# A hybrid decoder layer on one core: quarter sums of x made among the attention pairs, splits ordered behind bank copies, mixer weights split in the memory gates, mixer begun by halves

## The chip, the cores and the metric

The kernel runs on one core of one Trainium2 chip, and the metric is the device time of one execution in microseconds, where less is better. A core has TensorE (PE, the matrix products; its weight loads are listed as PEld), VectorE (DVE), ScalarE (ACT), GpSimd (POOL) and SyncE (SP), which each work through a list of their own in order. SP and POOL also issue the DMA transfers of this kernel. Products land in PSUM, in eight banks of 128 x 512 float32 numbers.

## The reference

The layer takes x (512 tokens of 1024) and a memory of 256 rows, all in float32:

```python
u = rms_norm(h, ln_mix_pre[l])
proj = jnp.einsum('bsd,de->bse', u, w_in[l])
qa, ka, va, qb, kb, vb, qm, gl = jnp.split(proj, split_idx, axis=-1)
y_swa = swa_sink_attention(...)        # banded, 8 heads in 2 key groups, sinks, relative bias
y_sb = stick_breaking_attention(...)   # 8 heads
y_mem = memory_cross_attention(...)    # 4 heads over 256 memory rows
g = jax.nn.sigmoid(gl.reshape(B, S, N_BRANCH, D))
merged = (g[:, :, 0] * jnp.einsum('bse,ed->bsd', y_swa, w_branch_swa[l])
          + g[:, :, 1] * jnp.einsum('bse,ed->bsd', y_sb, w_branch_sb[l])
          + g[:, :, 2] * jnp.einsum('bse,ed->bsd', y_mem, w_branch_mem[l]))
mix = jnp.einsum('bsd,de->bse', merged, w_out[l])
h = h + rms_norm(mix, ln_mix_post[l])
u = rms_norm(h, ln_ffn_pre[l])
a = jax.nn.silu(jnp.einsum('bsd,df->bsf', u, w_gate[l])) * jnp.einsum('bsd,df->bsf', u, w_up[l])
ffn = jnp.einsum('bsf,fd->bsd', a, w_down[l])
h = h + rms_norm(ffn, ln_ffn_post[l])
```

## The kernel before, in words

**Products in three.** TensorE multiplies in a float32 form of reduced width (`F32R`). Every operand is therefore split into a high part (a cast on ScalarE) and a low part (raw minus high, on VectorE), by `split` (L134), and a product is made as three (`mm3`, L166 to L170): high by high, high by low, low by high. `after(ins, first)` (L180) adds an ordering edge: `ins` comes later than `first` where both stand on one engine's list.

**The stream.** A `Stream` (L33) holds units in a list. A unit has a weight to load, its split, and a generator that issues its products and says how many microseconds of TensorE each piece is worth. `ahead` runs loads four units ahead and splits three ahead (two for the last branch weights); `begin` functions of a unit run just before its products. `run(us)` issues so many microseconds of products, and `until(flag)` runs to a marked unit. The attention heads are generators as well: they issue their scores and softmax, then give a number of microseconds for the stream's products to fill, then go on with transposes and outputs. The program is written in this order, and a planner then makes each engine's list from it by its own estimates, with the earlier written work first where both are ready.

**Order of the stages.** Projections for the stick-breaking heads come first, then those heads (`sb_head`, L824) among the remaining projections, the memory keys and values and the stick-breaking branch's gates. Then four pairs of banded heads (`swa_pair`, `yield 10.0` and `yield 2.0`) run among `qm` (four units), the stick-breaking branch (`branch_sb`, four units) and the first gate units. Then come the two memory pairs (`mem_pair`) among the banded branch's gates and products, then the memory branch's gates and products, the mixer, and the feed-forward network.

**Gates by quarters.** The banded and the memory branch's gates (1024 x 1024 weights) are multiplied by a scheme of seven products of quarters in place of eight: p1, p2, p5, p3, p6, p7, p4 (`QUART`), each with two units (c = 0, 1) of 12 products (`quart`), 2.7 us. Left sides are quarters of u or sums of quarters of the scaled x (`q_sum1` to `q_sum4`: scalings on ScalarE, L467, and accumulating DMAs issued by POOL); `q_parts` splits those sums. Right sides are quarters of the weight; the later ones are made by accumulating DMAs over the raw tile of an earlier one (`q_issue`, L449), which must wait until that one has been split. p1, p6, p7 and p4 go on in the banks called x, p5 and p3 in y, p2 in w; where a bank is gone on with, its state is first copied out by ScalarE (`q_end`, L534). In the banded branch the quarter sums serve both branches' gates: x quarters are loaded when the weights of units 2 and 3 of the gates are loaded, and sums and splits hang on the units -1 to 7, counted from the first gate unit (`g0`).

**Branches, merge, mixer.** `branch_t` multiplies the banded and memory outputs by the branch weights for each half h of the columns and each of four token tiles t, multiplies by the gate on VectorE (L583), and for the memory branch adds the banded branch's part on POOL or, for the last tile, on VectorE (L586). `merge(h)` transposes the sum on TensorE (L597), adds the stick-breaking part on VectorE (L601) and splits the result into `merged` (tiles `mgh`, `mgl`). `mix(t)` multiplies a token tile by the two halves of `w_out` (eight `mm3` each), and goes on with norm and residual. The mixer's weights are loaded into the stream's staging buffers (`wp`, four of each kind) and split by `out_load` and `out_split` after the flag `gates_late`.

**Memory.** Nearly all tiles of 128 x 512 come from one pool of 71 (`ckp`). PSUM has two pools, of two banks (`dps`) and six (`aps`).

Of the kernel before, what the change touches and what calls it, by code (L numbers as in the profile page):

```python
# [105 lines left out]
def tile_kernel(ctx, tc, a):  # L106
# [3 lines left out]
    ckp = ctx.enter_context(tc.tile_pool(name="ckp", bufs=71))  # L110
# [55 lines left out]
    def mm3(out, l, r, start, stop):  # L166
        (lh, ll), (rh, rl) = l, r
        nc.tensor.matmul(out, lh, rh, start=start, stop=False, skip_group_check=True)  # L168
        nc.tensor.matmul(out, lh, rl, start=False, stop=False, skip_group_check=True)  # L169
        nc.tensor.matmul(out, ll, rh, start=False, stop=stop, skip_group_check=True)  # L170
# [330 lines left out]
    def q_parts(p):  # L501
        for c in range(2):
            t = quarter.pop((p, c))
            if p == "p7":

                for k in range(2):
                    h, l = cols(u[2 * c + k], 256, 256)
                    split(t[:, k * 256 : (k + 1) * 256], h, l)
            else:
                qsum[(p, c)] = parts(f"xs{p}{c}", t)  # L510
# [19 lines left out]
    def q_end(b, p, i):  # L530
        ps = qbank[(QBANK[p], i)]
        if p in ("p1", "p5", "p6", "p7"):
            t = qkeep[(p, i)] = ck(f"gq{b}{p}{i}")
            nc.scalar.copy(t[:, :], ps[:, :])  # L534
# [16 lines left out]
    def quart(b, p, c):  # L551
        def gen(hi, lo):
            for i in range(2):
# [4 lines left out]
                for k in range(2):  # L558
                    mm3(qbank[key][:, :], q_left(p, c, k, i), cols((hi, lo), k * 512, 512), first and k == 0, c == 1 and k == 1)
# [6 lines left out]
    def branch_t(b, h, q):  # L566


        def gen(hi, lo):
# [3 lines left out]
            for t in range(NT):  # L573
# [10 lines left out]
                if b == MEM:  # L584
                    eng = nc.vector if t == NT - 1 else nc.gpsimd
                    eng.tensor_tensor(g[:, :], g[:, :], gate_t[(SWA, t, h)][:, :], op=ALU.add)  # L586
                    if (h, t) == (1, 0):
# [4 lines left out]
    def merge(h):  # L592

        for c in range(4):
            pt = aps(f"mg{h}{c}")
# [1034 lines left out]
```

## Time and profile before

| | |
|---|---|
| Median of three runs | 807.53 us (807.14 to 809.06) |
| The profiled execution | 808.21 us |
| Its span, first to last instruction | 806.4 us |
| Mean granted TensorE clock in it | 0.999 |
| TensorE busy | 792.4 us, 98% |
| VectorE, ScalarE, GpSimd busy | 608.1, 474.5, 106.4 us |
| DMA | 123.43 MB, 149 GB/s over the span |

The profile is of one execution, with the time of every instruction on every engine. A row of the groups has the line of the kernel that issued it, the engine, the operation, the tiles written and read (numbers of buffers left out), the shape and the count; then the busy time and the mean, and the idle time of the engine ahead of it with what ended it. Rows in order of time begin with start and duration in us. The ends of matrix products are modelled, so that the busy time of TensorE overstates how full it is; the distances between starts tell more. The 128 x 512 products that follow each other undisturbed start 0.23 us apart. The granted clock was full in all slices of the page.

### The profile page before, as it was taken

To read this page: it belongs to the slowest core of one execution; us is meant where nothing else is said; L and a number is where in the kernel's file an instruction comes from. 1 tells how busy PE (TensorE), PEld (TensorE's weight loads), DVE (VectorE), ACT (ScalarE), POOL (GpSimd) and SP (SyncE) were. 2 spreads that over 40 slices of the span, in tenths; PEclk is the share of its full clock that TensorE was granted. 3 is DMA by queue.
4 is the path that set the end of the run, shared out by engine and by line. 5 is a ranking of instruction groups with operands and counts; after the bars stand their busy time and mean duration, and the time that the engine had idled before them with its cause. 6 is when DMAs were issued, how large, how long until landed. Compare 5 with 4: busy or idle time off the path is not lost.

```text
span 806.4 us, 12444 instructions
## 1 busy us (share of the span) xinstructions
PE 792.4 (98%) x4694; PEld 695.6 (86%) x4694; DVE 608.1 (75%) x957; ACT 474.5 (59%) x847; POOL 106.4 (13%) x131
## 2 busy tenths in 40 slices
PE   9999999999999989999999999999999999999996
PEld 6899888778788868888778899999999999988885
DVE  6994877556588866775787579877676767898797
ACT  7562776556655686565844466654444444666673
POOL 1203200000000240002044200110000000205200
PEclk9999999999999999999999999999999999999999
DMA  8444535121123798339789806987767662859802
GB/s 296 141 128 134 185 105 157 54 78 53 53 79 105 158 193 204 91 70 176 255 275 304 156 1 174 265 203 203 190 179 192 171 170 74 192 124 228 202 0 104
DMA packets 41724, 123.43 MB, mean 153 GB/s; under 512 B 4928, under 2 KB 6640, under 8 KB 41664
## 3 DMA queue, kind: packets, MB, share of 16 engines
q1 hardware_dynamic: 29760, 86.32, 33.3%
q0 software_dynamic: 11472, 35.93, 24.1%
q8 instruction: 36, 0.59, 0.3%
q10 hardware_dynamic: 432, 0.39, 0.1%
q14 instruction: 24, 0.20, 0.1%
HBM read 116.85 MB, written 3.67 MB: 149 GB/s over the span
## 4 chain that ended last, share of the span: by engine, by line
PE 90%; DMA 3%; DVE 3%; issue 2%; ACT 1%; POOL 0%; DVEq 0%; POOLq 0%; ACTq 0%
PE gx L168 5%; PE gx L170 5%; PE gx L169 5%; PE z L173 4%; PE gy L170 3%; PE gy L168 3%; PE gy L169 3%; PE x L170 2%; PE x L169 2%; PE x L168 2%; PE br L169 2%; PE br L168 2%; PE br L170 2%; PE mx L170 2%; PE mx L169 2%
## 5 line engine op out<-in xcount | busy, mean ns | idle before, releaser
L136 ACT CAST hi<-gw 128x1024 fp32r<-128x1024 f32 x77 | 79.9, 1048 | 83.0 <-DVE gw L1212 39.6
L137 DVE TENSOR_TENSOR lo<-raw,hi 128x1024 fp32r<-128x1024 f32 (+2 forms) x76 | 91.9, 1210 | 41.1 <-ACT hi L136 41.1
L137 DVE TENSOR_TENSOR lo<-gw,hi 128x1024 fp32r<-128x1024 f32 x77 | 93.5, 1223 | 33.2 <-ACT hi L136 33.0
L136 ACT CAST hi<-raw 128x1024 fp32r<-128x1024 f32 (+2 forms) x76 | 78.4, 1037 | 55.5 <-PE pv L170 10.5
L1194 POOL DMA_DIRECT2D gw<-in_w_gu x27 | 23.3, 939 | 195.7 <-DMA gw<-in_w_gu 60.7
L136 ACT CAST hi<-r 128x1024 fp32r<-128x1024 f32 (+1 forms) x24 | 23.6, 982 | 19.8 <-PE y L170 5.3
L169 PE MATMUL x<-lo,lh 128*128 128x512 f32 x88 | 34.3, 389 | 0.0
L168 PE MATMUL x<-hi,lh 128*128 128x512 f32 x88 | 34.2, 389 | 0.0
L170 PE MATMUL x<-hi,ll 128*128 128x512 f32 x88 | 34.1, 390 | 0.0
L137 DVE TENSOR_TENSOR lo<-r,hi 128x1024 fp32r<-128x1024 f32 (+1 forms) x24 | 27.1, 1131 | 3.6 <-ACT hi L136 3.5
L186 ACT ACTIVATE e<-e 128x384 f32<-128x384 f32 (+1 forms) x48 | 26.9, 561 | 1.5
L137 DVE TENSOR_TENSOR lo<-bp,hi 128x512 fp32r<-128x512 f32 x33 | 22.6, 720 | 5.9 <-ACT hi L136 5.8
L136 ACT CAST hi<-bp 128x512 fp32r<-128x512 f32 x33 | 19.3, 620 | 13.1 <-PE y L170 4.8
L449 POOL DMA_DIRECT2D raw<-in_w_g x16 | 14.6, 976 | 90.8 <-DVE lo L137 74.1
L858 DVE SCALAR_TENSOR_TENSOR e<-z,e 128x384 f32<-128x384 f32 (+1 forms) x24 | 14.3, 598 | 15.7 <-ACT e L186 15.7
L170 PE MATMUL mx<-woh,mgl 128*128 128x512 f32 x64 | 25.1, 392 | 0.4 <-DVE mgl L137 0.4
L168 PE MATMUL g<-uh,hi 128*128 128x512 f32 x64 | 25.4, 398 | 0.0
L170 PE MATMUL g<-uh,lo 128*128 128x512 f32 x64 | 25.3, 396 | 0.0
L168 PE MATMUL gx<-B11h,hi 128*128 128x256 f32 x88 | 25.1, 285 | 0.2 <-ACT B11h L1123 0.2
L168 PE MATMUL mx<-woh,mgh 128*128 128x512 f32 x64 | 25.1, 392 | 0.0
L168 PE MATMUL gx<-T4h,hi 128*128 128x256 f32 x88 | 25.1, 285 | 0.0
L169 PE MATMUL g<-ul,hi 128*128 128x512 f32 x64 | 25.0, 391 | 0.0
(672 smaller groups left out, 2833.1 us busy)
## 6 DMA issues: line engine op xcount, KB each, us to landing
gw<-in_w_gu SPq DMA_DIRECT2D x57, 512.0 KB, 5.0
gw<-in_w_gu POOLq DMA_DIRECT2D x27, 512.0 KB, 7.5
raw<-in_w_p SPq DMA_DIRECT2D x22, 512.0 KB, 3.7
raw<-in_w_g POOLq DMA_DIRECT2D x16, 512.0 KB, 6.3
raw<-in_w_g SPq DMA_DIRECT2D x12, 512.0 KB, 3.7
bp<-in_w_dn SPq DMA_DIRECT2D x22, 256.0 KB, 10.9
r<-in_w_dn POOLq DMA_DIRECT2D x10, 512.0 KB, 8.8
raw<-in_w_brt SPq DMA_DIRECT2D x8, 512.0 KB, 4.1
```

What stands on the lines that cost most here:

```text
L136: ins = nc.scalar.copy(hi, raw)
L137: lows = nc.vector.tensor_tensor(lo, raw, hi.bitcast(F32), op=ALU.subtract)
L168: nc.tensor.matmul(out, lh, rh, start=start, stop=False, skip_group_check=True)
L169: nc.tensor.matmul(out, lh, rl, start=False, stop=False, skip_group_check=True)
L170: nc.tensor.matmul(out, ll, rh, start=False, stop=stop, skip_group_check=True)
L173: return nc.tensor.matmul(out, l, r, start=start, stop=stop, skip_group_check=True)
L186: ins = nc.scalar.activation(*args, **kw)
L449: nc.gpsimd.dma_start(t[:, :], src, accum_op=ALU.add)
L858: nc.vector.scalar_tensor_tensor(x, z[i][:, :n], 0.0, x, op0=ALU.max, op1=ALU.add)
L1194: nc.gpsimd.dma_start(gw[(n, key)][:, :], g_src(n, i, j), accum_op=ALU.add)
```

## The change

It makes no other numbers and no other products. It moves work and adds ordering edges:

- The pool of 128 x 512 tiles has 73 in place of 71.
- The x quarters are loaded at the begin of the units ten and nine ahead of the first banded gate unit, and `q_sum1` to `q_sum4` hang on the units eight to five ahead (the four `qm` units).
- `q_parts` handles one half c at a time, on units 1 to 8, and each split is ordered behind the last copy of a bank (`st["chain"]`). `q_end` now notes its copy there, and `w_split`, which already ordered its cast behind `st["chain"]` in the stick-breaking heads, follows it.
- The gate and branch products by quarters are put in a chain by `mm3_behind`: each group of three is ordered behind the one before it.
- `merge(0)` comes after token tile 1 of the memory branch's second half, not after tile 0, and two banks of `merge(1)` come from the pool of two.
- The flag `gates_late` is set after the memory gates' p2, not p6. `w_out` is loaded into tiles of the big pool, in the order of its rows (both halves h for one q, then the next q), with 2.6 us of products between a load and its split and 2.6 after it, instead of 2.5 after both.
- The mixer multiplies the first four blocks of rows for token tile 0, then `merge(1)`, the first four for tile 1, then the last four of either; tiles 2 and 3 follow whole.

```diff
-    ckp = ctx.enter_context(tc.tile_pool(name="ckp", bufs=71))
+    ckp = ctx.enter_context(tc.tile_pool(name="ckp", bufs=73))
...
     def mm3(out, l, r, start, stop):
         (lh, ll), (rh, rl) = l, r
-        nc.tensor.matmul(out, lh, rh, start=start, stop=False, skip_group_check=True)
+        one = nc.tensor.matmul(out, lh, rh, start=start, stop=False, skip_group_check=True)
         nc.tensor.matmul(out, lh, rl, start=False, stop=False, skip_group_check=True)
-        nc.tensor.matmul(out, ll, rh, start=False, stop=stop, skip_group_check=True)
+        return one, nc.tensor.matmul(out, ll, rh, start=False, stop=stop, skip_group_check=True)
+
+    def mm3_behind(*args):
+
+        one, last = mm3(*args)
+        if "products" in st:
+            after(one, st["products"])
+        st["products"] = last
...
-    def q_parts(p):
-        for c in range(2):
-            t = quarter.pop((p, c))
-            if p == "p7":
-
-                for k in range(2):
-                    h, l = cols(u[2 * c + k], 256, 256)
-                    split(t[:, k * 256 : (k + 1) * 256], h, l)
-            else:
-                qsum[(p, c)] = parts(f"xs{p}{c}", t)
+    def q_parts(p, c):
+        t = quarter.pop((p, c))
+        if p == "p7":
+
+            for k in range(2):
+                h, l = cols(u[2 * c + k], 256, 256)
+                after(split(t[:, k * 256 : (k + 1) * 256], h, l), st["chain"])
+        else:
+            h, l = qsum[(p, c)] = ck(f"xs{p}{c}h", F32R), ck(f"xs{p}{c}l", F32R)
+            ins = split(t[:, :], h[:, :], l[:, :])
+            if "chain" in st:
+                after(ins, st["chain"])
...
         if p in ("p1", "p5", "p6", "p7"):
             t = qkeep[(p, i)] = ck(f"gq{b}{p}{i}")
-            nc.scalar.copy(t[:, :], ps[:, :])
+
+            st["chain"] = nc.scalar.copy(t[:, :], ps[:, :])
...
-                    mm3(qbank[key][:, :], q_left(p, c, k, i), cols((hi, lo), k * 512, 512), first and k == 0, c == 1 and k == 1)
+                    mm3_behind(qbank[key][:, :], q_left(p, c, k, i), cols((hi, lo), k * 512, 512), first and k == 0, c == 1 and k == 1)
...
-                    mm3(ps[:, :], (yh[:, tok], yl[:, tok]), w, k == 0, k == 3)
+                    mm3_behind(ps[:, :], (yh[:, tok], yl[:, tok]), w, k == 0, k == 3)
...
-                    if (h, t) == (1, 0):
+                    if (h, t) == (1, 1):
                         merge(0)
...
-            pt = aps(f"mg{h}{c}")
+            pt = (dps if (h, c) in ((1, 0), (1, 1)) else aps)(f"mg{h}{c}")
...
-            if (b, p) == (MEM, "p6"):
+            if (b, p) == (MEM, "p2"):
                 dn.mark("gates_late")
...
-                (2, "load", x_quarters, (1, 1)),
-                (2, "load", x_quarters, (0, 1)),
-                (3, "load", x_quarters, (0, 0)),
-                (3, "load", x_quarters, (1, 0)),
-                (-1, "begin", q_sum1, ()),
-                (0, "begin", q_sum2, ()),
-                (2, "begin", q_sum3, ()),
-                (2, "begin", q_parts, ("p5",)),
-                (4, "begin", q_parts, ("p3",)),
-                (4, "begin", q_sum4, ()),
-                (6, "begin", q_parts, ("p6",)),
-                (7, "begin", q_parts, ("p7",)),
+                (-10, "begin", x_quarters, (1, 1)),
+                (-10, "begin", x_quarters, (0, 1)),
+                (-9, "begin", x_quarters, (0, 0)),
+                (-9, "begin", x_quarters, (1, 0)),
+                (-8, "begin", q_sum1, ()),
+                (-7, "begin", q_sum2, ()),
+                (-6, "begin", q_sum3, ()),
+                (-5, "begin", q_sum4, ()),
+                (1, "begin", q_parts, ("p5", 0)),
+                (2, "begin", q_parts, ("p5", 1)),
+                (3, "begin", q_parts, ("p3", 0)),
+                (4, "begin", q_parts, ("p3", 1)),
+                (5, "begin", q_parts, ("p6", 0)),
+                (6, "begin", q_parts, ("p6", 1)),
+                (7, "begin", q_parts, ("p7", 0)),
+                (8, "begin", q_parts, ("p7", 1)),
...
     def out_load(h, q):
-        src = a["w_out"][:, h, 2 * q : 2 * q + 2].rearrange("p k n -> p (k n)")
-        st[("wo", h, q)] = w_load(src, 1024)
+        st[("wo", h, q)] = []
+        for k in (2 * q, 2 * q + 1):
+            t = ck(f"wo{h}{k}")
+            nc.sync.dma_start(t[:, :], a["w_out"][:, h, k])
+            st[("wo", h, q)].append(t)
...
+    def mix_mm(t, k0, k1):
+        tok = slice(t * P, (t + 1) * P)
+        if k0 == 0:
+            mixed[t] = [aps(f"mx{t}{h}") for h in range(2)]
+        order = [(h, k) for h in range(2) for k in range(k0, k1)] if k0 == 0 else [(h, k) for k in range(k0, k1) for h in range(2)]
+        for h, k in order:
+            x = (merged[k][0][:, tok], merged[k][1][:, tok])
+            mm3(mixed[t][h][:, :], x, cols(wo[(h, k)], 0, 512), k == 0, k == KC - 1)
...
-    outs = [(h, q) for h in range(2) for q in range(4)]
+    outs = [(h, q) for q in range(4) for h in range(2)]
     dn.until("gates_late")
     for i, (h, q) in enumerate(outs):
         out_load(h, q)
+        dn.run(2.6)
         out_split(h, q)
-        dn.run(2.5)
+        dn.run(2.6)
...
+    mix_mm(0, 0, 4)
+    merge(1)
+    mix_mm(1, 0, 4)
+    mix_mm(0, 4, KC)
     tmp[0] = mix(0)
+    mix_mm(1, 4, KC)
     fs.ahead(2, -1)
     tmp[1] = mix(1)
```

More of the change, by code (lines that the diff above doesn't have):

```diff
@@ L1038, in out_load @@
     def out_load(h, q):
-        src = a["w_out"][:, h, 2 * q : 2 * q + 2].rearrange("p k n -> p (k n)")
-        st[("wo", h, q)] = w_load(src, 1024)
-    def out_split(h, q):
-        raw = st.pop(("wo", h, q))
-        for i in range(2):
-            k = 2 * q + i
-            wh, wl = ck(f"woh{h}{k}", F32R), ck(f"wol{h}{k}", F32R)
-            split(raw[:, i * 512 : (i + 1) * 512], wh[:, :], wl[:, :])
-            wo[(h, k)] = (wh[:, :], wl[:, :])
+        st[("wo", h, q)] = []
[3 more added lines that the diff above has]
+            st[("wo", h, q)].append(t)
+    def out_split(h, q):
+        for k, t in zip((2 * q, 2 * q + 1), st.pop(("wo", h, q))):
+            wo[(h, k)] = parts(f"wo{h}{k}", t)
     def rstd_small(name, ss):
@@ L1067, in x_load @@
             nc.sync.dma_start(hres[t][h][:, :], a["x"][t * P : (t + 1) * P, h * 512 : (h + 1) * 512])
-    def mix(t):
-        tok = slice(t * P, (t + 1) * P)
-        xr = hres[t]
-        ps = [aps(f"mx{t}{h}") for h in range(2)]
-        order = [(h, k) for h in range(2) for k in range(4)] + [(h, k) for k in range(4, 8) for h in range(2)]
-        for h, k in order:
-            if (t, h, k) == (0, 1, 0):
-                merge(1)
-            mm3(ps[h][:, :], (merged[k][0][:, tok], merged[k][1][:, tok]), wo[(h, k)], k == 0, k == KC - 1)
+    mixed = {}
+    def mix_mm(t, k0, k1):
[6 more added lines that the diff above has]
+            mm3(mixed[t][h][:, :], x, cols(wo[(h, k)], 0, 512), k == 0, k == KC - 1)
+    def mix(t):
+        if t > 1:
+            mix_mm(t, 0, KC)
+        xr, ps = hres[t], mixed[t]
         ss, ss2 = small(f"ssm{t}", 2), small(f"ssh{t}", 2)
```

## The prediction

> **What bounds the kernel now.** I read the page first, then the list of who waited for whom on TensorE, then the time order of the engines round each wait.
>
> ```profile
> span 806.4 us, 12444 instructions
> PE 792.4 (98%) x4694; PEld 695.6 (86%) x4694; DVE 608.1 (75%) x957; ACT 474.5 (59%) x847; POOL 106.4 (13%) x131
> ```
>
> TensorE is the bound, and the change takes no product away. All that it can win is time in which TensorE stood still. The list of waits says where that was (total, times, longest, in us):
>
> ```profile
> PE g0p L168 <- ACT gq0p L534: 2.0, 1, 2.0
> PE mg L597 <- DVE gq2p L586: 1.2, 1, 1.2
> PE z L173 <- DVE sl L864: 1.1, 1, 1.1
> PE br L169 <- DVE lo L137: 0.5, 1, 0.5
> PE ysw L173 <- ACT pts L954: 0.5, 1, 0.5
> PE mx L170 <- DVE mgl L137: 0.4, 1, 0.4
> ```
>
> Five of the six lie in the stages that the diff edits (`z` belongs to the stick-breaking heads). In TensorE's own order (start, duration, then idle before it in brackets):
>
> ```profile
> 286.85 0.43 PE L173 MATMUL ysw<-pts,v_all 128*64 128x256 f32 x1 [0.52 <-ACT pts L954]
> ...
> 298.92 0.28 PE L170 MATMUL ms<-mks0h,qms0l 128*128 128x256 f32 x1
> 301.25 0.50 PE L168 MATMUL g0p<-hi,xsp30h 128*128 128x512 f32 x1 [2.05 <-ACT gq0p L534]
> ...
> 391.12 0.73 PE L168 MATMUL br<-hi,y20h 128*128 128x512 f32 x2
> 392.38 0.50 PE L169 MATMUL br<-lo,y20h 128*128 128x512 f32 x1 [0.53 <-DVE lo L137]
> ...
> 412.79 1.64 PE L597 MATMUL mg<-c_ident,gq2p 128*128 128x128 f32 x13 [1.16 <-DVE gq2p L586]
> ...
> 422.44 0.39 PE L168 MATMUL mx<-woh,mgh 128*128 128x512 f32 x1
> 422.67 0.39 PE L169 MATMUL mx<-wol,mgh 128*128 128x512 f32 x1
> ...
> 425.79 0.51 PE L170 MATMUL mx<-woh,mgl 128*128 128x512 f32 x1 [0.44 <-DVE mgl L137]
> ```
>
> The brackets sum to 0.52 + 2.05 + 0.53 + 1.16 + 0.44 = 4.70 us. A wait costs more than its bracket: from 298.92 to 301.25 are 2.33 us, where a 256-wide product normally takes about 0.12 (half of the 0.23 between the 512-wide ones at 422.44 and 422.67), so 2.21 for a bracket of 2.05. With 0.16 for each of five, **5.5 us** are there to be won.
>
> **The change, part by part.**
>
> *Quarter sums moved up.* Each wait has its cause on ScalarE, POOL and SP:
>
> ```profile
> 280.40 1.31 ACT L467 ACTIVATE xq<-xq,g_neg 128x256 f32<-128x256 f32 x3
> 281.61 3.29 ACT L467 ACTIVATE xq<-xq,xg 128x256 f32<-128x256 f32 x8
> ...
> 285.75 0.57 ACT L534 COPY gq0p<-g0p 128x512 f32<-128x512 f32 x1
> 286.22 0.58 ACT L954 COPY pts<-pt 128x512 f32<-128x512 f32 x1
> ...
> 297.18 1.05 ACT L136 CAST hi<-raw 128x1024 fp32r<-128x1024 f32 x1 [1.88 <-DMA raw<-in_w_g]
> ...
> 299.67 1.04 ACT L136 CAST hi<-raw 128x1024 fp32r<-128x1024 f32 x1 [0.62 <-DMA raw<-in_w_g]
> 300.62 1.07 ACT L534 COPY gq0p<-g0p 128x512 f32<-128x512 f32 x2
> ```
> ```profile
> 288.96 0.86 POOL L491 DMA_DIRECT2D xq<-xq  x1 [2.39 <-DMA xq<-xq]
> ...
> 290.03 2.45 POOL L449 DMA_DIRECT2D raw<-in_w_g  x2
> ```
> ```profile
> 270.68 0.33 SPq L148 DMA_DIRECT2D raw<-in_w_g  x1
> 271.11 1.80 SPq L462 DMA_DIRECT2D xq<-in_xq  x4
> ```
>
> The last four loads of x quarters stood in SP's queue until 271.11. Their scalings (L467, 0.41 us each by the x8 row) then held ScalarE when pair 3's transposes wanted copying (286.22): the 0.52. The sums made from them held POOL until 290.03, so p6's weights landed late and p6's two casts sat on ScalarE (297.18, 299.67) in front of the copies of p5's banks, which p3 overwrites: the 2.05. Afterwards the loads are issued ten and nine units ahead, and all 20 scalings and 2 negations among pairs 0 and 1. That is 20 x 0.41 + 2 x 0.57 (taking a negation like the copy at 285.75) = 9.3 us of ScalarE, and eight POOL and eight SP issues, moved. Room for them:
>
> ```profile
> 216.00:234.00 18.00, 18.00 (x103) 14.80 (x102) 14.65 (x34) 11.05 (x27) 0.41 (x2) 1.00 0.30 88
> 234.00:252.00 18.00, 18.00 (x106) 14.93 (x105) 15.23 (x35) 9.28 (x25) 0.41 (x2) 1.00 0.27 80
> ...
> 370.00:380.00 10.00, 10.00 (x45) 8.28 (x45) 5.04 (x5) 5.87 (x8) 2.69 (x4) 1.00 1.03 195
> 400.00:411.00 11.00, 11.00 (x50) 9.10 (x49) 11.00 (x13) 7.63 (x12) 5.46 (x3) 1.00 0.85 296
> ```
>
> (Columns: length, then busy PE, PEld, DVE, ACT, POOL, clock, DMA share, GB/s.) ScalarE is free for 6.95 + 8.72 = 15.7 us, POOL nearly all the time, DMA at 0.3. So 9.3 fit, but ScalarE comes to some 82% busy with softmaxes on it that transposes wait for. Cost between 0 (each scaling fills a gap) and 8.2 us (every scaling ahead of something that TensorE wants); before, 11 of them in one block cost 0.52, so I take **+0.5**. POOL's small fills of score tiles now queue behind eight issues of 0.86 each; POOL was busy for 0.41 us in either window, so that is nothing. Gain: both waits, 0.68 + 2.21 = **-2.9**; without this cover, 0.
>
> *Splits behind copies of banks.* The first p6 weight's split is still written ahead of p5's copies, so for it the edge does nothing and only the earlier DMA helps; the second's now comes behind them, which alone saves the second cast and its wait (0.62 + 0.95). What waits behind a held split is the same weight's subtraction and its products three units (8 us) on: nothing. For the memory branch's first weight it is two units, 5.4 us, against a cast of 1.05 and a subtraction of the same width: covered by some 3.
>
> *Products in a fixed order* (`mm3_behind`). It adds no instruction. It forbids what the trace shows at 391.12, a branch product in the middle of gate products; it also forbids filling a stall so. Between -0.2 and +0.5; I take 0.
>
> *Mixer weights in the gates.*
>
> ```profile
> 385.29 0.33 SPq L148 DMA_DIRECT2D raw<-in_w_out  x1
> 389.01 0.33 SPq L148 DMA_DIRECT2D raw<-in_w_brt  x1
> ```
>
> The second branch weight goes out at 389.01 because `w_out` takes the staging buffers in turn with it. With `w_out` in small tiles of its own it can go at 385.29 or before, which is over 3 us for a bracket of 0.53: **-0.7**. The splits start six units (16 us) sooner, at 5.2 us a step, so some six steps of eight are done by 400 and five of nine subtractions leave the stretch 400 to 411, in which VectorE was busy for 11.00 of 11. Those stretched subtractions were ahead of the addition that the first merge waited for:
>
> ```profile
> L137 DVE TENSOR_TENSOR wol<-raw,woh x16: 674/684/1782, 386.9 to 412.7; 128x512 fp32r<-128x512 f32 x16
> L137 DVE TENSOR_TENSOR mgl<-g,mgh x8: 675/682/1781, 420.5 to 433.0; 128x512 fp32r<-128x512 f32 x8
> 419.30 0.62 ACT L136 CAST mgh<-g 128x512 fp32r<-128x512 f32 x1 [3.44 <-POOL gq2p L586]
> ```
>
> The merge also moves behind 12 more products (2.7 us), so its 1.16 goes twice over: **-1.3**. The price is DMA: at 370 to 380 the engines are already full (1.03) with p5 to p4 weights, and 1 MB more comes in. Between 0 and one repeat of p6's late cast (2.2); casts run three units ahead, I take 0.
>
> *Mixer by halves.* Same 64 x 3 products. Token tile 0 needs the second merge only after 48 products (10.9 us) instead of 24. The 0.44 came from the first merge: one of its casts waited 3.44 us for a tile of the pool to come free, and two tiles more (73 for 71) mend that: -0.6. Against it, that merge now has 24 + 9 products (7.5 us) ahead of its last use where it had 36 + 9. VectorE needs in that time four sums and four subtractions at 0.68 and two gate products, 6.8 us, or 11.2 if each subtraction takes 1.78. So 0 to 3.7 too late; the median is 0.682, I take **+0.5**. [...] Tile 0's result comes 24 products (5.5 us) later; its transposes hide that:
>
> ```profile
> 443.86 1.41 DVE L1089 SCALAR_TENSOR_TENSOR mt<-xr,r_h,bc_g_fpre 128x512 f32<-128x512 f32 x2
> 457.60 1.04 PE L1135 MATMUL ut<-c_ident,mt 128*128 128x128 f32 x8
> ```
>
> 12 us of cover. The first feed-forward loads queue behind loads of x that come some 5 us later in the branch. They take no time from TensorE: the traffic by slices of 20.2 us shows that they were done a whole slice (the 24th, 464 to 484, with 1 GB/s) before the next began.
>
> ```profile
> GB/s 296 141 128 134 185 105 157 54 78 53 53 79 105 158 193 204 91 70 176 255 275 304 156 1 174 265 203 203 190 179 192 171 170 74 192 124 228 202 0 104
> ```
>
> **Sum.** -2.9 - 0.7 - 1.3 - 0.6 + 0.5 + 0.5 = -4.5 us: span 801.9. The profiled execution took 808.21, 1.8 over its span; the median of the runs is 807.53, 0.7 less. So **803.0 us**, its own range 800.8 (neither new cost, and the `z` wait of 1.1 gone through the larger pool) to 805.1.
>
> **Rivals.**
>
> *p6's casts stay in front* (0.12). The first is not tied behind the copies, and if its weights still land late, 2.2 us return: 805.2. For: the edge misses it. Against: POOL has no sums to issue by then.
>
> *The mixer waits instead* (0.10). Subtractions at 1.78: 3.2 us return, 806.2. For: the maximum of 1781 on these very tiles. Against: the median.
>
> *Nothing moves* (0.06). The edges and the new places bind the planner, which lists each engine's order from its estimates; it may set equal waits elsewhere: 807.5.
>
> *ScalarE in pairs 0 and 1 becomes the bound* (0.17). A scaling ahead of an exponential or of a copy of transposes delays the pair, and TensorE's order is fixed. If all 8.2 us are exposed: 803.0 - 0.5 + 8.2 = 810.7. It is slower than before once 5.0 of them (12 of 20) are. For: the 11 in a block at 280.40; and my count of live tiles of the pool in these pairs (u 16, gates 8, SB outputs 8, biases 4, keys 4, queries 6, memory keys and values 8, quarters 10, scores 4, memory queries 5) is 73 of 73, so one tile more also delays a softmax. Against: the 15.7 free us, and products of `qm` that no edge ties.
>
> **Numbers.** 0.55 for the forecast, 0.45 for the rivals as given. 0.3% (2.4 us) is about what can be told from no change: faster is under 805.1, slower over 809.9. The first two rivals fall just over 805.1; some of their spread, 0.05, lies under. So faster 0.60, same 0.23, slower 0.17. The range runs from 800.8 to 810.2: it leaves out hardly anything below, and the full exposure above.
>
> **What would show it.** `g0p <- ACT gq0p`, `ysw <- ACT pts`, `br <- DVE lo` and `mg <- DVE gq2p` are gone from TensorE's waits; the L467 rows lie before 250; no POOL issue of `xq` after 260. Wrong would be: new waits of `pt` or `ysw` between 215 and 260, of `g0p` on its copy, or of `mx` on `mgl` above 1 us.

## The result and the profile after

| | before | after |
|---|---|---|
| Median beside each other | 807.53 us | 803.16 us (802.10 to 803.96) |
| Ratio with its 95% interval | | 0.9942 [0.9924, 0.9959] |
| Median beside each other, timed again on another occasion | 808.82 us | 803.67 us |
| Ratio of that | | 0.9940 [0.9927, 0.9953] |
| The profiled execution | 808.21 us | 803.96 us |
| Its span | 806.4 us | 801.9 us |

The change makes the kernel 4.4 us faster. The forecast was 803.0 us, with a span of 801.9. These are the first lines of the page of after:

```profile
span 801.9 us, 12466 instructions
...
PE 791.9 (99%) x4694; PEld 695.8 (87%) x4694; DVE 608.0 (76%) x957; ACT 474.8 (59%) x847; POOL 105.2 (13%) x131
```

Work is the same within half a microsecond on TensorE, VectorE and ScalarE; only waiting went. The list of who waited for whom on TensorE after (total, times, longest, in us), complete:

```profile
PE warm L180 <- DVE idle L728: 1.4, 1, 1.4
PE z L180 <- DVE sl L878: 1.1, 1, 1.1
PE mx L170 <- DVE mgl L137: 0.3, 1, 0.3
PE x L168 <- ACT lh L136: 0.3, 1, 0.3
PE gx L168 <- ACT B11h L1142: 0.2, 1, 0.2
```

The warm-up, `z` and `gx` were there before. Of the five waits that the prediction went for, four are gone and `mx` is left. A wait of `x` in the feed-forward network is new.

Where the time went is read from the starts of the same product in both traces. A stage's gain is the change of the difference across it (a minus is a gain):

| The start of | before, us | after, us | difference | across the stage |
|---|---|---|---|---|
| first product of `kb` | 22.86 | 23.25 | +0.39 | +0.39 (ahead of every edit) |
| last `pt` of the banded pairs | 283.32 | 284.15 | +0.82 | **+0.43**: heads and pairs |
| first `br` on `y00` | 324.58 | 321.67 | -2.91 | **-3.73**: banded gates |
| first `ut` | 457.60 | 452.26 | -5.35 | **-2.44**: memory gates, branch, merge, mixer |
| 22nd `w`, in the down-projection | 783.89 | 779.36 | -4.53 | **+0.82**: feed-forward network |

The first row is chance: over the fourteen traces of this document that product starts between 22.27 and 23.25. The second holds the stick-breaking heads as well; counted from the first score product `s` of the pairs, the loss in the pairs is 0.41, and the losses in the pairs of the kernels below are counted so.

In the banded gates, TensorE's and ScalarE's rows round the old wait, in order of time (after):

```profile
294.56 1.05 ACT L136 CAST hi<-raw 128x1024 fp32r<-128x1024 f32 x1 [0.94 <-PE g0p L170]
...
295.88 0.59 ACT L544 COPY gq0p<-g0p 128x512 f32<-128x512 f32 x1 [0.26 <-PE g0p L170]
...
297.04 0.39 PE L168 MATMUL g0p<-hi,xsp30h 128*128 128x512 f32 x1
...
297.24 0.59 ACT L544 COPY gq0p<-g0p 128x512 f32<-128x512 f32 x1 [0.77 <-PE g0p L170]
...
297.72 1.05 ACT L136 CAST hi<-raw 128x1024 fp32r<-128x1024 f32 x1
```

The copy of p5's bank is done 0.57 us before p3's first product starts. Of the two casts of p6's weights the first, at 294.56, is through before the first copy, and the second comes behind both copies. The moved operations, grouped (nanoseconds as least, median and most, then first and last start):

```profile
L474 ACT ACTIVATE xq<-xq,xg x12: 492/494/498, 214.2 to 229.7; 128x256 f32<-128x256 f32 x12
...
L474 ACT ACTIVATE xq<-xq,g_neg x8: 493/498/513, 213.4 to 227.7; 128x256 f32<-128x256 f32 x8
...
L506 POOL DMA_DIRECT2D xq<-xq x2: 892/1060/1229, 235.6 to 236.2; - x2
```

All scalings have started by 230 and POOL issues its last sum at 236.2. What that did to ScalarE is in the windows (length, then busy PE, PEld, DVE, ACT and POOL, clock, DMA share, GB/s):

```profile
216.00:234.00 18.00, 18.00 (x103) 14.79 (x102) 15.03 (x34) 17.61 (x44) 4.17 (x7) 1.00 0.56 121
234.00:252.00 18.00, 17.91 (x102) 14.46 (x101) 14.70 (x34) 9.46 (x26) 3.37 (x7) 1.00 0.61 141
...
400.00:411.00 11.00, 11.00 (x55) 9.23 (x54) 7.30 (x11) 0.05 (x1) 4.32 (x4) 1.00 0.77 228
```

ScalarE is busy for 17.61 of 18 us in the first of them, where it was 11.05. VectorE, full before from 400 to 411, has 3.70 us free there. The merge and the mixer after, in order of time:

```profile
409.96 1.91 PE L607 MATMUL mg<-c_ident,gq2p 128*128 128x128 f32 x16
...
417.08 1.93 POOL L1047 TENSOR_SCALAR bc_g_post<-bc_g_post 128x512 f32<-128x512 f32 x1
...
418.98 3.10 POOL L1047 TENSOR_SCALAR bc_g_fpre<-bc_g_fpre 128x512 f32<-128x512 f32 x2
...
419.20 0.93 DVE L137 TENSOR_TENSOR mgl<-g,mgh 128x512 fp32r<-128x512 f32 x1
...
420.19 0.50 PE L170 MATMUL mx<-wo03h,mgl 128*128 128x512 f32 x1 [0.34 <-DVE mgl L137]
```

The first merge runs its 16 transposes without a stop. The wait of `mx` is still there, for the last low part of that merge.

### The profile page after: what moved, and what is told of

Same layout as the page of the kernel before. It is cut to its first block, busy times and chain, and to the rows that moved or that the text cites. A ratio compares the mean times of both kernels' runs of the same rounds, so it can differ in the third digit from the quotient of the medians.

```text
span 801.9 us, 12466 instructions
## 1 busy us (share of the span) xinstructions
PE 791.9 (99%) x4694; PEld 695.8 (87%) x4694; DVE 608.0 (76%) x957; ACT 474.8 (59%) x847; POOL 105.2 (13%) x131
## 4 chain that ended last, share of the span: by engine, by line
PE 88%; DVE 5%; DMA 3%; issue 2%; ACT 1%; POOL 1%; DVEq 0%; POOLq 0%; ACTq 0%
PE gx L168 5%; PE gx L170 5%; PE gx L169 5%; PE z L180 4%; DMA bp<-in_w_dn 3%; PE gy L170 3%; PE gy L168 3%; PE gy L169 3%; PE br L168 3%; PE br L169 3%; PE br L170 3%; PE mx L170 2%; PE mx L169 2%; PE mx L168 2%; PE g L168 2%
## 5 line engine op out<-in xcount | busy, mean ns | idle before, releaser
L872 DVE SCALAR_TENSOR_TENSOR e<-z,e 128x384 f32<-128x384 f32 (+1 forms) x24 | 14.3, 597 | 15.7 <-ACT e L193 15.7
L170 PE MATMUL gy<-N22h,lo 128*128 128x256 f32 x88 | 25.0, 284 | 0.0
L168 PE MATMUL gy<-N22h,hi 128*128 128x256 f32 x88 | 25.0, 284 | 0.0
```

The lines of the kernel that those rows point to most:

```text
L168: one = nc.tensor.matmul(out, lh, rh, start=start, stop=False, skip_group_check=True)
L170: return one, nc.tensor.matmul(out, ll, rh, start=False, stop=stop, skip_group_check=True)
L872: nc.vector.scalar_tensor_tensor(x, z[i][:, :n], 0.0, x, op0=ALU.max, op1=ALU.add)
```

## The experiments

My theory was the prediction's: the moved quarter sums take away the waits of `ysw` and `g0p`, `w_out` in tiles of its own takes away `br`, the later merge with freed VectorE takes away `mg`, and two tiles more take away `mx`; the ordering edges are worth nothing. The rivals were that the edges do the work, that some part costs what others win, and that ScalarE in the pairs is about to become the bound. Each part was put alone into the kernel before (the four others with the pool of 73); the five together are the changed kernel. Ratios are to the kernel before on the same chip at the same time.

**The pool alone.**

```diff
-    ckp = ctx.enter_context(tc.tile_pool(name="ckp", bufs=71))
+    ckp = ctx.enter_context(tc.tile_pool(name="ckp", bufs=73))
```

> The kernel before with 73 tiles in the big pool in place of 71, nothing else. My theory (each wait has its own cause, the pool matters only for the first merge's cast that waited 3.44 us for a tile): between 806.9 and 807.7 us; TensorE's waits for gq0p (2.0), pts (0.5), lo (0.5) and gq2p (1.2) all still there. Rival (the waits come from a full pool): two or more of these waits gone and 803 to 805 us.

Measured: 808.65 us against 808.01, ratio 1.0009 [1.0000, 1.0017]. The waits of `g0p` (2.0), `mg` (1.2) and `br` (0.5) stay, and `mx` on `mgl` is 0.4 as before. So two tiles more don't mend that wait, and the -0.6 that I gave them was put to the wrong edit. The wait of `ysw` (0.5) is not in this list, nor in that of the mixer's edits alone, though the sums are at their old place in both; with the edges alone and with `w_out` alone it is there (0.4 and 0.5). So it changes with the execution. The execution in the profile shows something else beside, which the last section takes up.

**The quarter sums moved, with the pool of 73, and no ordering edge.**

```diff
...
+                (-10, "begin", x_quarters, (1, 1)),
+                (-10, "begin", x_quarters, (0, 1)),
+                (-9, "begin", x_quarters, (0, 0)),
+                (-9, "begin", x_quarters, (1, 0)),
+                (-8, "begin", q_sum1, ()),
+                (-7, "begin", q_sum2, ()),
+                (-6, "begin", q_sum3, ()),
+                (-5, "begin", q_sum4, ()),
                 (2, "begin", q_parts, ("p5",)),
...
```

> The kernel before with 73 tiles and the x quarters and quarter sums at their new places, splits where they were, no new edges. My theory (the late sums hold ScalarE, POOL and so p6's weights): the waits ysw on pts (0.5) and g0p on gq0p (2.0) go, 0.5 us comes back in the pairs: 807.5 - 2.9 + 0.5 = 805.1 us, from 804.4 to 805.6. Rival (p6's casts stay in front of p5's copies without an edge): g0p still waits 2.0, 806.9 to 807.3. Rival (ScalarE in pairs 0 and 1 becomes the bound): new waits of pt or ysw between 215 and 260 us, up to 8 us in all, 807 to 813.

Measured: 805.48 us, ratio 0.9969 [0.9957, 0.9981]. The banded gates gain 3.73 us by the starts of the same products, as in the whole change, and the pairs lose 0.63. The memory stage, which this part doesn't touch, loses 0.42. ScalarE's order, without any edge to a copy:

```profile
295.95 0.59 ACT L534 COPY gq0p<-g0p 128x512 f32<-128x512 f32 x1 [0.26 <-PE g0p L170]
...
297.31 0.59 ACT L534 COPY gq0p<-g0p 128x512 f32<-128x512 f32 x1 [0.77 <-PE g0p L170]
...
297.80 1.05 ACT L136 CAST hi<-raw 128x1024 fp32r<-128x1024 f32 x1
```

They are the rows of after, 0.07 us later. The planner sets the second cast behind the copies here without an edge. The moved sums are the whole gain of this stage.

**The edges alone**: splits behind copies of banks, `q_parts` by halves, products in a fixed order; the sums stay where they were.

```diff
-            nc.scalar.copy(t[:, :], ps[:, :])
+            st["chain"] = nc.scalar.copy(t[:, :], ps[:, :])
...
-                    mm3(qbank[key][:, :], q_left(p, c, k, i), cols((hi, lo), k * 512, 512), first and k == 0, c == 1 and k == 1)
+                    mm3_behind(qbank[key][:, :], q_left(p, c, k, i), cols((hi, lo), k * 512, 512), first and k == 0, c == 1 and k == 1)
...
```

> The kernel before with 73 tiles, the splits of weights and quarter sums ordered behind the copies of banks (quarter-sum splits one half at a time) and the products in a chain; the quarter sums stay late. My theory: p6's first cast is not tied and stays in front, the second is tied behind p5's copies, so 1.6 of the 2.2 us go, and the pts wait (0.5) stays: 805.4 to 806.4 us with g0p waiting about 0.5. Rival (the edges do it all, the moved sums are not needed): g0p's wait gone entirely, 804.8 to 805.3. Rival (a fixed order of products takes away TensorE's way round a wait): slower than 807.5.

Measured: 809.73 us, ratio 1.0019 [1.0009, 1.0029], slower. The wait of `g0p` falls from 2.0 to 1.3 and the banded gates gain 1.25 us, but the memory stage loses 2.85. It has a wait that was not there before, 3.3 us in two pieces. The first of them:

```profile
388.71 1.04 ACT L136 CAST hi<-raw 128x1024 fp32r<-128x1024 f32 x1
...
389.66 0.61 ACT L136 CAST woh<-raw 128x512 fp32r<-128x512 f32 x1
...
390.18 0.58 ACT L543 COPY gq2p<-g2p 128x512 f32<-128x512 f32 x1
...
390.81 0.50 PE L168 MATMUL g2p<-hi,uh 128*128 128x512 f32 x1 [1.23 <-ACT gq2p L543]
```

p4 waits for p7's bank, whose copy stands behind two casts on ScalarE. In the kernel before, TensorE made branch products at this place (391.12 in the prediction's rows). The fixed order forbids them. I had expected this kernel to gain some 1.6 us; the last rival of the expectation came true. The prediction put the fixed order between -0.2 and +0.5: the mechanism was named, and its size was far off for a kernel in which `w_out` still goes through the staging buffers. About 1.6 of the 2.85 us are a lower clock behind the second piece (last section). The splits behind copies are in this kernel too, so the 2.85 aren't the fixed order's alone by this run.

**`w_out` in tiles of the pool alone**, split from p2 on, with 73 tiles.

```diff
-        src = a["w_out"][:, h, 2 * q : 2 * q + 2].rearrange("p k n -> p (k n)")
-        st[("wo", h, q)] = w_load(src, 1024)
+        st[("wo", h, q)] = []
+        for k in (2 * q, 2 * q + 1):
+            t = ck(f"wo{h}{k}")
+            nc.sync.dma_start(t[:, :], a["w_out"][:, h, k])
+            st[("wo", h, q)].append(t)
...
-            if (b, p) == (MEM, "p6"):
+            if (b, p) == (MEM, "p2"):
...
```

> The kernel before with 73 tiles, w_out loaded to tiles of the pool and split from the memory gates' p2 on; merge and mixer as before. My theory: the wait of br on lo (0.5 and the refill, 0.7) goes, since the branch weight no longer takes turns with w_out for a staging buffer; the wait of mg on gq2p (1.2) shrinks to under 0.6, since five of nine subtractions leave the stretch before it: 805.8 to 806.8 us. Rival (DMA at 370 to 380 was full, 1 MB more makes p6's weights late): a new wait of g2p of up to 2.2 us, 807 to 809.

Measured: 805.32 us, ratio 0.9965 [0.9953, 0.9978]. `br`, `mg` and `mx` are all gone from the waits, and the memory stage gains 2.79 us. The loads of the branch weights, the window that was full, and the merge, in this kernel:

```profile
381.43 2.95 SPq L148 DMA_DIRECT2D raw<-in_w_brt  x2
```
```profile
400.00:411.00 11.00, 11.00 (x50) 9.11 (x49) 8.96 (x11) 4.88 (x8) 4.25 (x3) 1.00 0.11 34
```
```profile
411.93 1.91 PE L597 MATMUL mg<-c_ident,gq2p 128*128 128x128 f32 x16
```

The second branch weight goes out right behind the first, at about 384 instead of at 389.01, as the prediction had it for `br`. VectorE is busy for 8.96 of 11 us in the window instead of 11.00, and the merge runs without a stop where it always stood. The later merge isn't needed for it. The tiles of its own and the earlier start of the splits are one edit here; neither was tried without the other.

**The later merge and the mixer by halves alone**, with 73 tiles.

```diff
-                    if (h, t) == (1, 0):
+                    if (h, t) == (1, 1):
                         merge(0)
...
+    mix_mm(0, 0, 4)
+    merge(1)
+    mix_mm(1, 0, 4)
+    mix_mm(0, 4, KC)
     tmp[0] = mix(0)
+    mix_mm(1, 4, KC)
...
```

> The kernel before with 73 tiles, the first merge behind token tile 1, two banks of the second merge from the pool of two, and the mixer begun by halves; nothing else. My theory: the first merge's wait (1.2) is covered by 12 more products, the wait on mgl (0.4) stays about as it is, everything before 391 us as before: ratio 0.9975 to 0.9995. Rival (it only helps with w_out split early, as w_out's stretched subtractions are what the merge waits for): the wait moves to mgl and grows past 1 us, ratio 0.9995 to 1.002.

Measured: 808.08 us against 808.52, ratio 0.9996 [0.9986, 1.0006], no gain that can be told from nothing. The wait of `mg` goes here as well, so either edit removes it, but the two others stay:

```profile
PE br L169 <- DVE lo L137: 0.5, 1, 0.5
...
PE mx L170 <- DVE mgl L137: 0.4, 1, 0.4
```

The memory stage gains 0.79 us. If the lost wait of `mg` is worth the 1.3 that the prediction gave it, 0.5 is left as the price of this part, of which 0.3 is a new wait of `br` on `gq2p`. The prediction took 0.5 for beginning by halves.

**The two useful parts together**: moved sums and `w_out` in tiles (the two diffs above), 73 tiles, no edge, merge and mixer as before.

> The kernel before with 73 tiles, the moved quarter sums and the w_out change; no ordering edges, products free, merge and mixer as before. Alone these two gave ratios of 0.9969 and 0.9965, and in their profiles they removed different waits. My theory of the prediction (all parts carry a term): 0.9945 to 0.9960, slower than the whole change by the merge's and mgl's terms. Rival (these two are all of the gain, the edges and the halves of the mixer carry nothing): 0.993 to 0.9945, the same as the whole change or better.

Measured: 802.19 us against 808.52, ratio 0.9920 [0.9907, 0.9933]. Its list of waits, without the warm-up and `gx`:

```profile
PE z L173 <- DVE sl L864: 1.1, 1, 1.1
PE pt L952 <- DVE w L941: 0.3, 1, 0.3
PE x L168 <- ACT lh L136: 0.2, 1, 0.2
```

The memory stage gains 2.95 us where the whole change gains 2.44. The rival of the expectation held: these two parts, with the two tiles, are all of the gain. This is less code than the change and no slower: the interval overlaps with that of the whole change (0.9940 [0.9927, 0.9953]), and the two weren't timed at the same time, so "faster" isn't claimed.

**The whole change without the fixed order of products** (`mm3` in place of `mm3_behind`).

```diff
-                    mm3_behind(qbank[key][:, :], q_left(p, c, k, i), cols((hi, lo), k * 512, 512), first and k == 0, c == 1 and k == 1)
+                    mm3(qbank[key][:, :], q_left(p, c, k, i), cols((hi, lo), k * 512, 512), first and k == 0, c == 1 and k == 1)
```

> The whole change without the chain of products (the gate and branch products are free to be set in another order by the planner), the splits still behind the copies. My theory (the chain of products is worth between -0.2 and +0.5 us, taken as 0): ratio 0.9935 to 0.995, no new wait above 0.5 us. Rival (the fixed order matters: in the run with edges alone it brought waits of 3.3 us of p4 on p7's copies): either those do not come back because w_out no longer stands in ScalarE's way, and it is the same; or without the order branch products get between gate products again and a wait of br on lo of 0.5 is back.

Measured: 802.90 us against 808.52, ratio 0.9928 [0.9915, 0.9941]. Nothing needed the fixed order. Its memory stage gains 2.41 us, the same as with it in the first trace of after, so with `w_out` in tiles of its own the order cost nothing in that execution. The second trace of after, below, gains less.

**Every scaling of a quarter made twice** (the whole change, with a second scaling by 1.0 behind each; the outputs stay the same).

```diff
             nc.scalar.activation(out[:, sl], x[:, sl], AF.Identity, scale=g[:, kk : kk + 1])
+            nc.scalar.activation(out[:, sl], out[:, sl], AF.Identity, scale=1.0)
```

> The whole change with every scaling of a quarter of x followed by a second one by 1.0 in place, same numbers: 20 more ScalarE instructions of about 0.41 us, 8.2 us, among pairs 0 and 1 (ScalarE was free for 15.7 us there, and the moved work takes 9.3 of it). My theory (the gaps hold them): the added time is 0 to 1.5 us, ratio 0.994 to 0.996, no wait above 1 us between 215 and 260. Rival (ScalarE in pairs 0 and 1 is about to become the bound): 3 to 8 us more, ratio 0.998 to 1.004, with waits of pt or ysw on pts or w there.

Measured: 808.90 us against 808.52, ratio 1.0003 [0.9993, 1.0013]. 20 small instructions take back the whole gain, as the rival said. The first row is a window, the other two are in order of time:

```profile
216.00:234.00 18.00, 18.00 (x91) 15.17 (x90) 12.67 (x30) 17.98 (x52) 3.54 (x4) 1.00 0.54 115
```
```profile
235.58 1.04 ACT L969 COPY pts<-pt 128x512 f32<-128x512 f32 x2
...
236.20 0.65 PE L180 MATMUL ysw<-pts,v_all 128*64 128x256 f32 x2 [1.61 <-ACT pts L969]
```

ScalarE is full in the window, and the pairs lose 6.06 us instead of 0.41. Of the 5.65 more, 1.61 are the wait in these rows and about 1.6 the lower clock behind it (last section); the rest stands in no wait of TensorE's list. So the rival that I gave 0.17 is right about the place: ScalarE in pair 0 is at its limit.

**The changed kernel again, and three neighbours of it, on one chip.**

> The changed kernel once more, beside the three below on one chip. My theory: ratio 0.993 to 0.995 to the kernel before (its first timing gave 0.9942), with a mix wait of 0.3 and an x wait of 0.3 at 757. The point is the comparison with the smaller edit: if the ordering edges, the later merge and the mixer by halves carry anything, this kernel is at least 0.8 us faster than the moved sums with w_out in tiles of 73; if they carry nothing or cost, it is level or up to 1.5 us slower. I expect 0 to 1.5 slower.

Measured: 803.67 us against 808.82, ratio 0.9940 [0.9927, 0.9953]. This execution has no loss in the feed-forward network, but one in the memory gates instead, whose stage gains only 1.23 us:

```profile
385.10 0.62 ACT L136 CAST wo12h<-wo 128x512 fp32r<-128x512 f32 x1 [0.71 <-DMA wo<-in_w_out]
...
387.70 1.06 ACT L544 COPY gq2p<-g2p 128x512 f32<-128x512 f32 x2
...
388.33 0.50 PE L168 MATMUL g2p<-hi,uh 128*128 128x512 f32 x1 [1.11 <-ACT gq2p L544]
```

TensorE came into this stage 0.96 us sooner than in the first trace of after (-3.87 against -2.91), the tiles of `w_out` didn't, and ScalarE's casts wait for them in front of the copy that p4 needs. This is the DMA bound of the prediction (0 to 2.2, taken 0): it is 0 in one execution and 1.1 in another. To come sooner is not enough for it: in the kernel without the fixed order TensorE is as early (-3.85), the same cast starts at 383.88 with no wait for a transfer, and this wait of `g2p` is not there. Whether the fixed order has a part in it, by keeping TensorE from branch products meanwhile, stays open.

**Without the splits behind copies** (`q_parts` by whole quarters at its old units and no edge; everything else of the change).

```diff
-                (1, "begin", q_parts, ("p5", 0)),
-                (2, "begin", q_parts, ("p5", 1)),
...
+                (2, "begin", q_parts, ("p5",)),
```

> The whole change without the splits behind copies of banks (q_parts by whole quarters at the old units, no edge to a copy; the fixed order of products stays). My theory: the moved sums alone bring p6's weights in time, so the copies need no edge: within 0.8 us of the whole change, and no wait of g0p or g2p on a copy of a bank above 0.5 us. Rival (the edges are what removes the 2.05): a wait of g0p on gq0p of 1 us or more comes back, and the time is 1.5 to 3 us above the whole change.

Measured: 803.30 us, ratio 0.9934 [0.9919, 0.9949], level with the whole change. No wait on a copy of a bank is in its list. The pairs lose 0.65 us here and 0.63 and 0.67 in the two kernels above without these splits, against 0.41 to 0.44 in the three traces with them. So 0.2 us is all that the splits by halves may bring, and the last kernel below loses nothing in the pairs without them.

**Moved sums and `w_out`, with the old 71 tiles.**

```diff
-    ckp = ctx.enter_context(tc.tile_pool(name="ckp", bufs=73))
+    ckp = ctx.enter_context(tc.tile_pool(name="ckp", bufs=71))
```

> Moved quarter sums and w_out in tiles of the pool, with the pool at 71 tiles as before. The point is what the two extra tiles do. My theory: w_out's 16 raw tiles and the x quarters held longer need them, so with 71 a tile comes free later: 0.5 to 2 us slower than with 73, seen as a wait of a cast or a load for a tile in pairs 0 and 1 or in the memory branch. Rival (the extra tiles carry nothing): within 0.5 us of the kernel with 73. If the loss of 0.8 at the down-projection (x on lh at 757) is gone with 71, it belongs to the larger pool; if it stays, it does not.

Measured: 805.56 us, ratio 0.9960 [0.9946, 0.9973]. That is more than the 0.5 to 2 us that I expected to lose. The pairs lose 3.55 us where they lose 0.67 with 73 tiles:

```profile
240.51 0.20 POOL L918 MEMSET w<- 128x128 f32 x1 [3.79 <-DMA xq<-xq]
...
248.67 1.13 PE L952 MATMUL pt<-c_ident,w 128*128 128x128 f32 x7 [2.86 <-DVE w L941]
```

A score tile `w` takes the place of a quarter, and its fill waits 3.79 us for the last accumulating DMA on that quarter. So the two extra tiles belong to the moved sums, and in this trace they are worth 2.9 us. The loss in the feed-forward network is 0.38 here.

**Moved sums and `w_out` with 73 tiles, and the weights' low parts behind those of the heads**, against the `z` wait.

```diff
-            nc.vector.tensor_tensor(sl[i][:, :n], x, sh[i][:, :n].bitcast(F32), op=ALU.subtract)
+            st["head_low"] = nc.vector.tensor_tensor(sl[i][:, :n], x, sh[i][:, :n].bitcast(F32), op=ALU.subtract)
...
+        if "head_low" in st:
+            after(st["low"], st["head_low"])
```

> Moved sums and w_out in tiles of 73, and the low part of a weight ordered behind the last low part of a stick-breaking head, so that it no longer stands on VectorE ahead of what z waits for (the 1.1 at 167). My theory: the wait of 1.06 at 168.3 goes and with it 1.2 us, a ratio of 0.9905 to 0.991, about 801 us where the kernel before takes 808.2; VectorE has the time, since the weight's products come units later. Rival: the edge holds back other low parts in the heads (eight heads, a subtraction of 1.22 behind each chain), and products of kb, g or qb wait for lo: 0.5 to 2 us given back, the time level with or above the kernel without the edge.

Measured: 802.75 us, ratio 0.9925 [0.9913, 0.9938], no better than without the edge (0.9920). The `z` wait is gone, and another of the same size stands in a head before it:

```profile
136.85 1.52 PE L176 MATMUL ysb<-e,v_all 128*64 128x128 f32 x12 [1.12 <-ACT e L189]
```

With the new edge the planner gives the products out in another order and reaches `ysb` sooner than its exponentials.

## Why the prediction was right

The time and the span came out as forecast (803.0 and 801.9), and the two mechanisms that carry the gain are the forecast ones: the late sums, and `w_out` late and in shared staging buffers. That the number fits to 0.2 us is luck in part, as the steps show.

- **TensorE is the bound, and only waits can be won**: right. Its busy time changed by 0.5 us, and the span by 4.5.
- **Moved sums, -2.9**: right in mechanism, too small. The stage gained 3.7 us in every kernel with them but the one with doubled scalings. The gaps between starts in before that go come to 3.3 of that (0.68 and 2.21, and about 0.1 at each of four changes of product); 0.4 stays open.
- **Their cost in the pairs, +0.5**: right (+0.43), but the reason that the range gave for it, 15.7 us of free ScalarE over two windows, was wrong. Nearly all of the scalings went into the first window, where 6.95 us were free, and filled 6.56 of them. A scaling alone takes 0.49 us, not the 0.41 that I took from rows that group several. Each by itself, 20 scalings of 0.49 and two negations of 0.62 make 11.1 us and not 9.3. The doubled scalings show that as many again cost 5.65 more, with the clock's loss of the last section among them.
- **73 tiles, -0.6 for the `mx` wait**: wrong edit. The row in the prediction names POOL's addition of `gq2p` as the end of the cast's wait of 3.44 us, which I read as a wait for a tile; with 73 tiles the same cast still waits 2.84 us for it. The pool alone leaves the wait of `mx` at 0.4, `w_out` in its own tiles removes it. My count of live tiles, which I used only for a rival, was the right reason: with 71 the score tiles wait 2.86 us.
- **Splits behind copies, nothing**: right, since the kernel without them is level.
- **Fixed order, 0 between -0.2 and +0.5**: right for the first trace of the whole change, which leaving it out changes by 0.03 us in the stage; the second trace is 1.2 us behind, and there the order's part is open. Together with the other edges alone it costs 2.85 us in the memory stage. I take it that the range held because `w_out` went elsewhere at the same time; no kernel with the fixed order and without that was run but the one with the edges alone.
- **`w_out`, -0.7 for `br` and, with the later merge, -1.3 for `mg`**: right in size, and one edit too many named. `w_out` alone removes `br`, `mg` and `mx` and gains 2.79 to 2.99 us in the four kernels that have it without the mixer's edits.
- **Mixer by halves, +0.5**: right. The memory stage gains 2.44, 2.41 and 2.06 us in three kernels with the mixer's edits and no new wait in the gates, against 2.79 to 2.99 without them, so these edits cost 0.4 to 0.9, if the ordering edges that each of the three kernels still has in part cost nothing. In after, two low parts of the first merge take 2.80 us for the two, beside POOL's addition (1.66 us from 415.45) and its scaling of the norm gains (1.93 from 417.08), and one takes 0.93 beside the scaling, against 0.68 undisturbed; `mx` waits for the last. The upper end of the prediction, 3.7 us too late, took 1.78 for each of the four. The stretch is there, but TensorE was held up for 0.34 us by it. How much of it comes from POOL was not shown.
- **DMA full at 370 to 380, 0 to 2.2, taken 0**: a term that changes from one execution to the next, 0 in the first trace and 1.1 in the second.
- **The feed-forward network, nothing**: wrong by 0.82 in the first trace. A wait of `x` on a cast of `lh` at about 757 us, up to 0.8 long, stands in eight of the thirteen traces of changed kernels, also where only the pool was changed, and the stage loses 0.75 to 1.33 us in each of them; with 71 tiles it loses 0.4 without such a wait. In the other four traces it loses nothing, among them the second trace of the same changed kernel. It hangs on the execution as well as on the kernel; its cause wasn't settled.

The sum in the first trace: +0.39 + 0.43 - 3.73 - 2.44 + 0.82 = -4.53. By the prediction it was -2.4 for the sums with their cost and -2.1 for the memory stage. So the total came out right partly by luck: 0.8 us of gain in the banded gates beyond the forecast met 0.8 of loss in the feed-forward network that no step had, and the 0.39 ahead of every edit was met by the 0.3 more in the memory stage.

## What to carry to other kernels

When many waits have causes on one queue, look for the one transfer or staging buffer that makes the others late: two of the five parts here, with the two tiles that one of them needs, carry the gain, and the ordering edges, the later merge and the mixer by halves bring nothing beside them. An edge that fixes an order can take away the planner's way round a stall, so price it in the kernel without its companions, too. Free time on an engine counts in the window into which the moved work will really go, not as a sum over neighbours, and work moved earlier needs the tiles that it holds for longer.

## What the hardware did that I had not expected

A long wait of TensorE can cost more than itself. The windows of the pool alone, and the products behind its wait of 2.02 us:

```profile
299.00:301.00 2.00, 0.66 (x3) 0.56 (x4) 1.68 (x4) 2.00 (x4) 0.73 (x1) 1.00 1.07 211
301.00:303.00 2.00, 2.00 (x7) 1.57 (x6) 1.83 (x5) 1.73 (x5) 0.86 (x1) 0.55 1.06 209
303.00:305.00 2.00, 2.00 (x7) 1.56 (x6) 1.72 (x4) 0.00 (x1) 0.00 (x0) 0.60 1.06 203
```
```profile
300.34 0.50 PE L168 MATMUL g0p<-hi,xsp30h 128*128 128x512 f32 x1 [2.02 <-ACT gq0p L534]
...
302.40 0.63 PE L168 MATMUL g0p<-hi,xsp30h 128*128 128x512 f32 x1
302.82 0.63 PE L169 MATMUL g0p<-lo,xsp30h 128*128 128x512 f32 x1
```

From 301.2 on the granted clock is 0.5 for 3.4 us (by the windows: 2 x 0.45 and 2 x 0.40 us lost, at a loss of 0.5, make 3.4), and the products start 0.42 us apart instead of 0.23. That is 8 products by 0.2, 1.6 us on top of the wait. The same drop, of the same length (the windows lose 1.7 us of clock in each), followed the waits of 2.30 us (`w_out` alone), 2.09 (the edges alone) and 1.61 (doubled scalings). It didn't follow the wait of 2.05 in before, behind which the clock is 1.00 in each stretch of 2 us up to 309, nor that of 2.0 with the mixer's edits alone, where the mean clock of the execution is 0.999 and 3.4 us at 0.5 would have taken 0.002 from it. So the length of a wait alone doesn't decide: 1.61 us was followed by the drop and 2.05 was not. What else does was not shown.

The mean granted clock of an execution shows such a drop only roughly, since a drop behind the last product counts in it too: in the profile of after the last product starts at 794.77, the clock is 0.50 from 800 on, and the mean is 0.998; the execution above has 0.997. In the kernel before the mean was 0.996 or less in 15 of 56 executions, with a mean span of 807.4 us against 806.3 in the others. In the kernels with moved sums and 73 tiles, the doubled scalings aside, it was never that low, and it was in three of six executions with 71 tiles, where `pt` waits for 2.86 us. I take the executions with so low a mean for ones with a drop between products. Then to remove the wait of 2 us also removes this loss from about a quarter of the executions or more; 1.1 us in 15 of 56 make an estimate of 0.3 us in the mean.
